# Last block of the down projection: the first product's pairs 9 to 11 behind the second's first two, and the last rows' transposes in front of the seventh's second half

## The chip, the cores and the metric

The kernel runs on one core of a Trainium2 chip. The metric is the device time of one execution in microseconds. Before the change three runs took 992.59, 992.81 and 992.83 us; the median is 992.81.

## What is computed

A decoder trunk of two layers over 512 tokens of width 1024, in float32. Layer 0 mixes tokens with causal pooling, layer 1 with windowed attention; each is followed by a SwiGLU feed-forward block with 2816 hidden features, and a last rmsnorm ends it. Cut to what matters here:

```python
def swiglu(h, w_gate, w_up, w_down):
    g = jnp.einsum('bsd,df->bsf', h, w_gate)
    u = jnp.einsum('bsd,df->bsf', h, w_up)
    return jnp.einsum('bsf,fd->bsd', jax.nn.silu(g) * u, w_down)

def reference(x, ...):
    for i in range(DEPTH):
        h = rmsnorm(x, norm_mix[i])
        y = pool_mixer(h, ...) if i % N_MIXERS == 0 else attn_mixer(h, ...)
        x = x + y
        h = rmsnorm(x, norm_ffn[i])
        x = x + swiglu(h, ffn_w_gate[i], ffn_w_up[i], ffn_w_down[i])
    return rmsnorm(x, norm_final)
```

## The kernel before

**Precision.** Every float32 operand is split into a high part (a cast to fp32r on ScalarE, ACT) and a low part (the difference, on VectorE, DVE). A product is three matmuls: high by high, high by low, low by high. For weights these are L170 (`whi`) and L174 (`wlo`); for activations L360 and L361. The weights' halves live in a ring of five tiles, so a cast waits until TensorE (PE) has finished with the weights five tiles earlier.

**The feed-forward block** (`ffn`, one call for each layer) takes each large matmul as a 2 by 2 block product with seven products instead of eight, numbered 0 to 6. Their operands are sums of blocks. Sums of weights are made by transfers that add to what is there (POOL's, L138 and L179) and by additions on DVE (L176, `vraw<-vraw,wraw`). Sums of activations are made on ACT and DVE.

Gate and up go through eleven groups of 256 hidden features, numbered 0 to 10. Group `n`'s product `i` is `("quad", n, i)` in the plan. Its accumulators are PSUM tiles, `pair0` to `pair3`, which hold two banks each. `paired_done` (L706 to L737) takes a finished product out: L724 and L725 after product 5, L728 and L729 after product 6, then silu and multiplication (L741, L742, L732, L736), the sums of the result (L652, L653, L661), and their split into `u_hi` and `u_lo`. Group 10 keeps its split in two tiles named `t`, which group 10's own operands held before (`open_u`, L641).

Down takes the groups back in three blocks, groups 0 to 2, 3 to 5 and 6 to 10, each again with seven products. Within a block the groups go two by two: a weight tile `z` serves groups `2z` and `2z + 1` of the block. In the last block `z` 0 is groups 6 and 7 (the title's pairs 7 and 8, counted from one), `z` 1 groups 8 and 9 (pairs 9 and 10), `z` 2 group 10 alone (pair 11). `z` 0 and 1 take 12 matmuls of 128x512 each, `z` 2 takes 6. `("down", 2, i, zs)` is product `i` for the tiles in `zs`; a full product is 30 matmuls. Product 0 goes into `pair0` and is copied to `pair2` when complete (L832); product 1 goes into `pair3`, the bank of group 10's product 5.

**What sets the order.** PE follows the order of the program; `_plan` (L52) writes the feed-forward block's part of it. The other engines are ordered by a scheduler from that same program and its priorities, and each then works strictly in its order. The weight queue follows the plan too: a load, cast and split is issued some steps ahead of its use. So a step that moves in the plan moves its load on SP's queue and its cast and split on ACT and DVE.

**Behind the plan**, products 5, 4, 3 and 6 of the last block are written out at the end of `ffn` (L915 to L948) with the residual sum (L840, L842: "flush"), the squares for the next norm (L323), the multiplication by the gain (L332) and the scaling by the inverse root (L351). In layer 0 (`not final`) the normed rows of blocks 2 and 3 are also turned there: `turn_block` does eight 128x128 transposes on PE (L357) and splits the result into `h` (L360, L361), block 2 by way of `pair3`, block 3 by way of `pair2`. Product 6 is done in two halves, rows of block 0 (`first`, 15 matmuls) and of block 1 (`second`, 15 matmuls).

Then layer 1's attention starts with `by_halves` (L1108): three projections for q and k, for the tokens of blocks 2 and 3 first. Between them the transposes of blocks 0 and 1 are put in (L1116), from the row tiles `wraw` and `odd_rows`, which L351 has scaled.

Of the kernel before, what the change touches and what calls it, by code (L numbers as in the profile page):

```python
# [51 lines left out]
def _plan():  # L52
    first = lambda n: [("quad", n, 0)] if n in PAIRED else []
    down = lambda b, i, *zs: ("down", b, i, zs or tuple(range((len(BLOCKS[b]) + 1) // 2)))
    steps = TWO + [("one", 2, i) for i in range(6)] + first(3) + [("one", 2, 6)]
    for n in PAIRED:
        steps += [("quad", n, i) for i in USED]
        ends = [("quad", n, 5), ("quad", n, 6)]
        if n in (3, 6):
            b = n // 3 - 1  # L60
            steps += [down(b, 0)] + ends + [down(b, i) for i in range(1, 6)] + first(n + 1) + [down(b, 6)]
        elif n == 10:
            steps += [down(2, 0, 0, 1)] + ends + [down(2, 1, 0), down(2, 0, 2), down(2, 1, 1, 2)]
            steps += [down(2, i) for i in (2, 5, 4, 3, 6)]
        else:
            steps += first(n + 1) + ends
    return steps


PLAN = _plan()  # L70
TOKENS = np.arange(S).reshape(J, R).T.reshape(-1)
BY_GROUP = [6, 7, 4, 5, 2, 3, 0, 1]
# [3 lines left out]
def trunk_kernel(ctx: ExitStack, tc: tile.TileContext, x_in, xT, gam, gains, consts, ident_d, w0, wT, w1, wv, w_down, out):  # L76
# [290 lines left out]
    def by_residue(b):  # L367

        n = P // R

        def places(h, half, tp):
            at = h[:, 4 * half : 4 * half + 4, :].rearrange("p c (r j) -> p c r j", r=R)
            return at[:, :, :, b * n : (b + 1) * n], tp.rearrange("p c (i r) -> p c r i", r=R)

        return places

    def turned(norm, shift, b, tps, order):

        hi, lo = tokens_at(shift)
        for half, tp in enumerate(tps):  # L380
            norm.turn(b, half, tp)
        for half, tp in enumerate(tps):
            (to_hi, src), (to_lo, _) = order(hi, half, tp), order(lo, half, tp)
            with tc.high_priority(URGENT):
                split(to_hi, to_lo, src)
# [192 lines left out]
    def ffn(layer, norm, third, nxt):  # L578
# [8 lines left out]
        with ExitStack() as fctx:  # L587
# [299 lines left out]
            final = layer == 1  # L887
# [3 lines left out]
            last = downs[2]  # L891
            p, r, _, q = last.accs[:4]
# [20 lines left out]
            turn_block = lambda b, pair: turned(norm, 0, b, [by_four(pair[:, n, :]) for n in range(2)], by_residue(b))  # L913
# [12 lines left out]
            ws = last.operands(6, every)  # L926
            first = last.places(every, (0,))
            last.matmuls(6, ws, first[:4], lambda t: p[:, 0, :], False)
            if not final:
                turn_block(2, r)  # L930
            last.matmuls(6, ws, first[4:], lambda t: p[:, 0, :], False)
            with tc.high_priority(URGENT):
                last.flush(6, p[:, 0:1, :], slice(0, 1))
            closed(1, (0,))
            ready_block(0)
            second = last.places(every, (1,))
            for n, cs in enumerate(HALVES if final else COLS[:1]):
                to = (A[0], r)[n][:, 1, : cs.stop - cs.start]
                if final:
                    last.matmuls(6, ws, second, lambda t: to, True, cs)  # L940
                else:
                    last.matmuls(6, ws, second[:2], lambda t: to, True, cs)
                    turn_block(3, q)
                    last.matmuls(6, ws, second[2:], lambda t: to, False, cs)
                with tc.high_priority(URGENT):
                    last.flush(6, to.unsqueeze(1), slice(1, 2), cs)
                norm.square(1, 1, junk, 2 + n if final else None)
                norm.gained(1, 1, 2 + n if final else None)  # L948
# [5 lines left out]
        return norm  # L954

    norm = ffn(0, norm, third, 1)


    with ExitStack() as actx:
# [24 lines left out]
        def rope(ps, t, name):  # L984
            a = aw.tile([P, S], F32, name="ropea")
            sw = aw.tile([P, S], F32, name="ropeb")
            nc.vector.stream_shuffle(sw, ps, PARTNER)
            nc.vector.tensor_mul(a, ps, cosr)
            nc.gpsimd.tensor_mul(sw, sw, sinr)
            out = aw.tile([P, S], F32, name=name, bufs=3)  # L990

            if t >= 3:
                nc.vector.tensor_add(out, a, sw)
            elif name == "k":
                nc.vector.tensor_add(out.rearrange("p (b r i) -> p b r i", b=4, r=R), blocks_of(a), blocks_of(sw))
            else:
                by_r = lambda z: z.rearrange("p (r j) -> p r j", r=R)
                nc.vector.tensor_add(out.rearrange("p (j r) -> p r j", r=R), by_r(a), by_r(sw))
            return out
# [130 lines left out]
        for t in range(8):  # L1130
            pq = pqk[2 * t] if t < 2 else project(j_qk[2 * t], h_hi, h_lo)
            q = rope(pq, t, "q")
# [172 lines left out]
        third = out_projection(j_wo, range(NC), m_hi, m_lo, norm, SHIFT, four, lambda: [sc_tile(), sc_tile()])  # L1305

    ffn(1, norm, third, 3)
    mm.close()

# [66 lines left out]
```

## Time and profile before

| | |
|---|---|
| median of 3 runs | 992.81 us |
| profiled execution | 993.18 us |
| its span | 991.40 us |
| PE busy | 981.2 us, 99% |
| VectorE busy | 786.3 us, 79% |
| ScalarE busy | 573.7 us, 58% |
| GpSimd busy | 124.5 us, 13% |
| granted TensorE clock | 0.998 |
| read from HBM | 159.85 MB |

The span is what the trace covers, from the first instruction to the end of the last; the profiled execution's own time is 1.78 us longer. PE is TensorE's matmuls, PEld its weight loads, SP the engine that issues most transfers. A row of the timeline gives the start and the length in us, the engine, the line in the code, the operation, what it writes and reads by the program's names, and in brackets the engine's idle time before it and what ended it. A row of stretches gives the bounds, the length and the busy time of the engines with their instructions. The last block of down lies at 385 to 441 us in layer 0 and at 930 to 981 us in layer 1.

### The profile page before, as it was taken

To read this page: it belongs to the slowest core of one execution; us is meant where nothing else is said; L and a number is where in the kernel's file an instruction comes from. 1 tells how busy PE (TensorE), PEld (TensorE's weight loads), DVE (VectorE), ACT (ScalarE), POOL (GpSimd) and SP (SyncE) were. 2 spreads that over 40 slices of the span, in tenths; PEclk is the share of its full clock that TensorE was granted. 3 is DMA by queue.
4 is the path that set the end of the run, shared out by engine and by line. 5 is a ranking of instruction groups with operands and counts; after the bars stand their busy time and mean duration, and the time that the engine had idled before them with its cause. 6 is when DMAs were issued, how large, how long until landed. Compare 5 with 4: busy or idle time off the path is not lost.

```text
span 991.4 us, 15359 instructions
## 1 busy us (share of the span) xinstructions
PE 981.2 (99%) x5914; PEld 869.8 (88%) x5914; DVE 786.3 (79%) x1088; ACT 573.7 (58%) x898; POOL 124.5 (13%) x124
## 2 busy tenths in 40 slices
PE   9999999999999999999999999999999999999997
PEld 7888999988988998789888899899998898899876
DVE  6475789898988888787887547479989798888876
ACT  5573666646765676573543544357664676567655
POOL 0002010010011111102111023101101001110110
PEclk9999999999999999999999999999999999999999
DMA  9557276579469876653211249526757946987662
GB/s 335 181 173 188 52 199 165 137 208 251 127 163 248 216 186 146 149 191 129 85 56 54 61 149 268 116 53 178 199 125 206 254 125 161 249 220 188 139 145 98
DMA packets 79465, 162.98 MB, mean 164 GB/s; under 512 B 6096, under 2 KB 6480, under 8 KB 79392
## 3 DMA queue, kind: packets, MB, share of 16 engines
q1 hardware_dynamic: 58544, 122.04, 37.3%
q0 software_dynamic: 20560, 39.69, 23.3%
q8 instruction: 46, 0.75, 0.3%
q14 instruction: 27, 0.22, 0.1%
q10 hardware_dynamic: 288, 0.27, 0.1%
HBM read 159.85 MB, written 2.13 MB: 163 GB/s over the span
## 4 chain that ended last, share of the span: by engine, by line
PE 93%; DVE 3%; ACT 2%; DMA 1%; issue 1%; POOL 0%; SPq 0%; DVEq 0%; ACTq 0%
PE pair L673 31%; PE pair L817 19%; PE p L699 5%; PE mm L263 4%; PE mm L264 4%; PE mm L265 4%; PE pair L699 4%; PE r L699 2%; PE early L484 2%; PE mm L402 2%; PE mm L404 2%; PE mm L403 2%; PE mm L699 1%; DVE wlo L174 1%; PE early L531 1%; PE tp L1083 1%
## 5 line engine op out<-in xcount | busy, mean ns | idle before, releaser
L174 DVE TENSOR_TENSOR wlo<-wraw,whi 128x1024 fp32r<-128x1024 f32 (+2 forms) x190 | 220.1, 1163 | 70.0 <-ACT whi L170 69.5
L170 ACT CAST whi<-wraw 128x1024 fp32r<-128x1024 f32 (+2 forms) x189 | 184.4, 980 | 155.6 <-issue 28.1
L170 ACT CAST whi<-vraw 128x1024 fp32r<-128x1024 f32 (+1 forms) x108 | 105.4, 980 | 114.7 <-DVE vraw L176 38.1
L174 DVE TENSOR_TENSOR wlo<-vraw,whi 128x1024 fp32r<-128x1024 f32 (+1 forms) x108 | 121.8, 1132 | 44.5 <-ACT whi L170 44.3
L673 PE MATMUL pair<-h,whi 128*128 128x512 f32 (+1 forms) x640 | 143.2, 349 | 0.0
L673 PEld LDWEIGHTS pair<-h,whi 128*128 128x128 f32 x640 | 109.1, 189 | 13.4
L673 PE MATMUL pair<-t,whi 128*128 128x512 f32 (+1 forms) x512 | 110.6, 337 | 0.0
L817 PE MATMUL pair<-whi,u_hi 128*128 128x512 f32 (+1 forms) x284 | 109.9, 387 | 0.0
L817 PE MATMUL pair<-wlo,u_hi 128*128 128x512 f32 (+1 forms) x284 | 109.9, 387 | 0.0
L817 PE MATMUL pair<-whi,u_lo 128*128 128x512 f32 (+1 forms) x284 | 109.7, 386 | 0.0
L673 PEld LDWEIGHTS pair<-t,whi 128*128 128x128 f32 x512 | 86.0, 190 | 8.4
L673 PE MATMUL pair<-h,wlo 128*128 128x256 f32 x512 | 89.2, 281 | 0.0
L673 PEld LDWEIGHTS pair<-h,wlo 128*128 128x128 f32 x512 | 76.1, 188 | 4.2
L138 POOL DMA_DIRECT2D wraw<-w x22 | 26.7, 1211 | 397.5 <-DMA wraw<-w 111.9
L176 DVE TENSOR_TENSOR vraw<-vraw,wraw 128x1024 f32<-128x1024 f32 (+1 forms) x66 | 75.2, 1139 | 0.7
L673 PE MATMUL pair<-t,wlo 128*128 128x256 f32 x384 | 71.9, 282 | 0.0
L263 PE MATMUL mm<-h,whi 128*128 128x512 f32 (+1 forms) x176 | 64.9, 369 | 0.0
L264 PE MATMUL mm<-h,whi 128*128 128x512 f32 (+1 forms) x176 | 63.6, 362 | 0.9 <-DVE h L361 0.9
L265 PE MATMUL mm<-h,wlo 128*128 128x512 f32 (+1 forms) x176 | 63.5, 361 | 0.0
L817 PEld LDWEIGHTS pair<-whi,u_lo 128*128 128x128 f32 x284 | 53.3, 188 | 10.9
L817 PEld LDWEIGHTS pair<-whi,u_hi 128*128 128x128 f32 x284 | 53.4, 188 | 10.4
L817 PEld LDWEIGHTS pair<-wlo,u_hi 128*128 128x128 f32 x284 | 53.4, 188 | 10.3
(346 smaller groups left out, 2043.4 us busy)
## 6 DMA issues: line engine op xcount, KB each, us to landing
wraw<-w SPq DMA_DIRECT2D x116, 512.0 KB, 4.7
wraw<-w_down SPq DMA_DIRECT2D x32, 512.0 KB, 4.1
vraw<-w SPq DMA_DIRECT2D x22, 512.0 KB, 4.9
wraw<-w POOLq DMA_DIRECT2D x22, 512.0 KB, 7.5
vraw<-w POOLq DMA_DIRECT2D x22, 512.0 KB, 9.2
wraw<-wT SPq DMA_DIRECT2D x16, 512.0 KB, 4.2
vraw<-w_down POOLq DMA_DIRECT2D x12, 512.0 KB, 7.4
wraw<-w_down SPq DMA_DIRECT2D x24, 256.0 KB, 3.2
```

What stands on the lines that cost most here:

```text
L138: nc.gpsimd.dma_start(dst, more, accum_op=ALU.add)
L170: nc.scalar.copy(hi[:, :n], raw[:, :n])
L174: nc.vector.tensor_sub(lo[:, :n], raw[:, :n], hi[:, :n].bitcast(F32))
L176: nc.vector.tensor_add(raws[into][:, :n], raws[into][:, :n], raws[more][:, :n])
L263: nc.tensor.matmul(ps, lhsT=whi, rhs=xhi, start=first, stop=False, **kw)
L264: nc.tensor.matmul(ps, lhsT=whi, rhs=xlo, start=False, stop=False, **kw)
L265: nc.tensor.matmul(ps, lhsT=wlo, rhs=xhi, start=False, stop=last, **kw)
L402: nc.tensor.matmul(ps, lhsT=xhi, rhs=w[0][:, k, :], start=first, stop=False)
L403: nc.tensor.matmul(ps, lhsT=xhi, rhs=w[1][:, k, :], start=False, stop=False)
L673: mat = lambda o, w, m, **kw: nc.tensor.matmul(o, lhsT=w, rhs=m, skip_group_check=True, **kw)
L699: nc.tensor.matmul(ps[:, g, :], lhsT=w[:, g, c, :], rhs=right[:, z, c, :], start=i in (0, 1, 3) and g + c + k == 0, stop=c == 3 and k == 2 ...
L817: nc.tensor.matmul(acc(t), lhsT=u, rhs=w, start=first, stop=n == len(places) - 1, skip_group_check=True)
```

## The change

```diff
@@ _plan, n == 10
-            steps += [down(2, 0, 0, 1)] + ends + [down(2, 1, 0), down(2, 0, 2), down(2, 1, 1, 2)]
+            steps += [down(2, 0, 0)] + ends + [down(2, 1, 0), down(2, 0, 1, 2), down(2, 1, 1, 2)]
             steps += [down(2, i) for i in (2, 5, 4, 3, 6)]
@@ ffn, the end
             last.matmuls(6, ws, first[4:], lambda t: p[:, 0, :], False)
+            if not final:
+                turn_block(3, q)
             with tc.high_priority(URGENT):
                 last.flush(6, p[:, 0:1, :], slice(0, 1))
...
                 to = (A[0], r)[n][:, 1, : cs.stop - cs.start]
-                if final:
-                    last.matmuls(6, ws, second, lambda t: to, True, cs)
-                else:
-                    last.matmuls(6, ws, second[:2], lambda t: to, True, cs)
-                    turn_block(3, q)
-                    last.matmuls(6, ws, second[2:], lambda t: to, False, cs)
+                last.matmuls(6, ws, second, lambda t: to, True, cs)
```

`ends` are group 10's products 5 and 6. The first part applies to both layers, the second to layer 0 alone. Lines of the code behind L942 have a number smaller by 3 in the changed kernel. No matmul, transfer, cast or sum is added or taken away.

On PE, at the start of the last block in layer 0 (`pair_1536` is `pair0`, `pair_1539` is `pair3`, `pair_1537` is `pair1`; + is the changed kernel's order), group 10's last two products come after the first weight tile of product 0:

```order
 L817 MATMUL pair_1536<-whi,u_lo 128x512
+L673 MATMUL pair_1539<-h,whi 128x512 x8
+L673 MATMUL pair_1539<-h,wlo 128x256 x8
+L673 MATMUL pair_1537<-t_1001,whi 128x512 x8
+L673 MATMUL pair_1537<-t_1001,wlo 128x256 x8
+L817 MATMUL pair_1539<-whi,u_hi 128x512
+L817 MATMUL pair_1539<-wlo,u_hi 128x512
+L817 MATMUL pair_1539<-whi,u_lo 128x512
```

The four L673 rows and product 1's first 12 matmuls, of which the last three rows are the beginning, stood 12 matmuls later; product 0's second tile now follows them, directly ahead of its third, which reads `t`.

On ACT, at the end of group 10 in layer 0 (L724 and L728 take out products 5 and 6, L360 casts the result into `t`, L735 loads the table for the norm's root), the order was:

```order
L724 COPY ct<-pair_1539 128x512
L741 ACTIVATE ct<-ct 128x2x256
L170 CAST whi<-vraw 128x1024
L728 COPY ct<-pair_1537 128x512
L360 CAST t_999<-ct 128x512
L170 CAST whi<-vraw 128x1024
L732 ACTIVATE ct<-ct 128x256
L735 ACT_TABLE_LOAD
L735 ACTIVATE tiny<-tiny 128x1
L832 COPY pair_1538<-pair_1536 128x1024
L360 CAST t_999<-ct 128x1280
```

and is now:

```order
L724 COPY ct<-pair_1539 128x512
L170 CAST whi<-vraw 128x512
L741 ACTIVATE ct<-ct 128x2x256
L728 COPY ct<-pair_1537 128x512
L732 ACTIVATE ct<-ct 128x256
L735 ACT_TABLE_LOAD
L735 ACTIVATE tiny<-tiny 128x1
L360 CAST t_999<-ct 128x512
L360 CAST t_999<-ct 128x1280
L170 CAST whi<-vraw 128x1024 x2
L832 COPY pair_1538<-pair_1536 128x1024
```

Both casts into `t` stand behind the table load now, and product 2's first two weight casts stand behind both of them.

On ACT, at the end of layer 0's feed-forward block (`pair_1539` holds block 2's turned rows, `pair_1538` block 3's; L323 squares, L351 scales, the L170 rows cast the q and k weights), the order from the first turned half on was:

```order
L360 CAST h<-pair_1539 128x16x32 x2
L170 CAST whi<-wraw 128x1024
L323 ACTIVATE keep,ss<-x 128x512
L360 CAST h<-pair_1538 128x16x32
L338 ACTIVATE s_4153<-ss 128x1
L170 CAST whi<-wraw 128x1024 x2
L360 CAST h<-pair_1538 128x16x32
L351 ACTIVATE wraw<-wraw,r_4154 128x1024
L323 ACTIVATE keep,ss<-x 128x512
```

and is now:

```order
L360 CAST h<-pair_1539 128x16x32
L360 CAST h<-pair_1538 128x16x32
L360 CAST h<-pair_1539 128x16x32
L323 ACTIVATE keep,ss<-x 128x512
L360 CAST h<-pair_1538 128x16x32
L338 ACTIVATE s_4165<-ss 128x1
L170 CAST whi<-wraw 128x1024 x3
L323 ACTIVATE keep,ss<-x 128x512
L351 ACTIVATE wraw<-wraw,r_4166 128x1024
```

The four casts into `h` moved ahead of all three weight casts; the scaling of `wraw` moved behind the third weight cast and behind block 1's square.

## The prediction

> **What bounds the kernel now.** I read the page first: its head, the busy shares and the chain that ended last.
>
> ```profile
> span 991.4 us, 15359 instructions
> PE 981.2 (99%) x5914; PEld 869.8 (88%) x5914; DVE 786.3 (79%) x1088; ACT 573.7 (58%) x898; POOL 124.5 (13%) x124
> ...
> PE 93%; DVE 3%; ACT 2%; DMA 1%; issue 1%; POOL 0%; SPq 0%; DVEq 0%; ACTq 0%
> ```
>
> TensorE (PE) has work for 99% of the span. So a reordering that keeps every matmul can win only where PE now waits, and the next view is who PE waits for over the whole run (us in total, times, longest).
>
> ```profile
> PE mm L264 <- DVE h L361: 0.9, 2, 0.5
> PE pair L817 <- ACT t L360: 0.4, 2, 0.2
> ```
>
> Both rows touch the edit. `t` holds the operands of group 10 that the moved product reads (one wait in each layer), and `h` at L361 is the low half of the turned rows (two waits in layer 0). Idle time understates such a wait, because matmuls are pipelined, so I measure the stretches themselves. The rows below give the stretch, its length, then the busy time of PE, PEld, DVE, ACT and POOL.
>
> ```profile
> 385.02:390.48 5.46, 5.46 (x26) 4.51 (x25) 3.99 (x5) 2.00 (x3) 1.48 (x2) 1.00 0.72 163
> 390.48:396.10 5.62, 5.62 (x34) 4.90 (x32) 4.27 (x6) 3.47 (x5) 0.89 (x2) 1.00 0.89 166
> 396.10:405.22 9.12, 8.76 (x38) 6.61 (x37) 7.04 (x11) 7.03 (x11) 2.40 (x2) 1.00 0.88 191
> 412.02:418.82 6.80, 6.80 (x31) 5.63 (x30) 4.85 (x6) 4.01 (x5) 0.00 (x0) 1.00 0.22 63
> 941.49:950.62 9.13, 8.77 (x39) 6.61 (x38) 7.05 (x11) 6.86 (x10) 2.41 (x2) 1.00 0.87 190
> ```
>
> The first is the first product's two weight tiles (24 matmuls), the second group 10's last two products, the third the 36 matmuls after them, the fourth a product of 30 without any wait. 6.80/30 is 0.227 us a matmul, so 36 should take 8.16 us. They take 9.12 in layer 0 and 9.13 in layer 1: **0.96 and 0.97 us are lost at `t`.**
>
> **Part 1, product 0's later pairs moved.** No matmul, cast or transfer is added or removed. With the same durations PE would stand, on the clock of before, so: 12 matmuls of product 0 from 385.02 to 387.75, group 10's last two to 393.37, 12 of product 1 to 396.10, then pairs 9 and 10 of product 0 to 398.82, and there the first matmul that reads `t`. Its high half is needed at 398.82, its low half two matmuls later at 399.27. Now when `t` is ready:
>
> ```profile
> 393.50 0.59 ACT L724 COPY ct<-pair 128x512 f32<-128x512 f32 x1 [0.33 <-PE pair L673]
> 394.88 0.63 ACT L741 ACTIVATE ct<-ct 128x512 f32<-128x512 f32 x1 [0.80 <-DVE ct L725]
> 396.36 0.58 ACT L728 COPY ct<-pair 128x512 f32<-128x512 f32 x1
> 398.55 0.62 ACT L360 CAST t<-ct 128x512 fp32r<-128x512 f32 x1 [1.60 <-DVE ct L652]
> 400.05 0.41 ACT L732 ACTIVATE ct<-ct 128x256 f32<-128x256 f32 x1
> 400.48 1.28 ACT L735 ACT_TABLE_LOAD   x1
> ...
> 395.48 0.69 DVE L176 TENSOR_TENSOR vraw<-vraw,wraw 128x512 f32<-128x512 f32 x1
> 397.83 0.68 DVE L652 TENSOR_TENSOR ct<-ct 128x512 f32<-128x512 f32 x1
> 398.43 0.68 DVE L729 SCALAR_TENSOR_TENSOR ct<-pair,ct 128x512 f32<-128x512 f32 x1
> 399.37 0.68 DVE L361 TENSOR_TENSOR t<-ct,t 128x512 fp32r<-128x512 f32 x1
> ```
>
> Group 10's last product ends 2.73 us earlier, at 393.37. In the new order ACT does L741 at 393.16, L728 at 393.70 (PE's end plus the 0.2 that L724 shows after 393.30). DVE follows with L742, L729, L652, each 0.60 start to start, L652 ending at 395.7. ACT does L732 at 395.1 and now has the table load and its tiny activation (1.4 us) in front of the cast, which starts at 396.97 and ends at 397.6. DVE reaches the low half at 397.86, behind a 0.62 L176, and ends at 398.55. That is 0.7 us before 399.27, so the wait goes. What is late next would be product 1's first matmul at 393.37, which overwrites the bank that L725 reads: I get L725's end at 392.7, again 0.65 to spare. Spent covers would cost their overrun one for one. Bounds of this step: 0 to 0.97 a layer; I take all of it.
>
> On SP's queue the loads for product 0's second tile and for group 10's last product change places:
>
> ```profile
> 361.27 0.37 SPq L136 DMA_DIRECT2D wraw<-w_down  x1
> ...
> 366.13 0.37 SPq L136 DMA_DIRECT2D wraw<-w  x1
> ```
>
> Even the later of the two lands, at the 7.8 us of the slowest transfer below, 16 us before PE reads either tile (390.57 and 396.10), so the swap costs nothing.
>
> The other weights are the doubtful side. Product 2's splits (L174) fall behind `t`'s larger low half, and each releases the accumulating POOL transfer (L179) that brings product 5's weights.
>
> ```profile
> 398.32 1.19 POOL L179 DMA_DIRECT2D vraw<-w_down  x1 [5.03 <-DVE wlo L174]
> ...
> DMA to landing us min/median/max: 6.6/6.6/6.6
> ...
> 405.06 1.06 ACT L170 CAST whi<-vraw 128x1024 fp32r<-128x1024 f32 x1 [0.46 <-DMA vraw<-w_down]
> ...
> DMA to landing us min/median/max: 7.8/7.8/7.8
> ...
> DMA to landing us min/median/max: 5.7/5.7/5.7
> ```
>
> The landings are of this transfer in layer 0, of its twin in layer 1, and of one of the same size at 377.5 with nothing beside it. Laid out in the new order, the first split of product 2 ends at 401.46 instead of 397.92, and the issue follows 0.4 later (as 398.32 follows 397.92), at 401.85. Landing at 6.6 is 408.5; the cast (1.06), the split (1.23, the L174 row further down) and 0.15 between make 410.9. Product 5 starts at 411.06 and reads the low half one matmul later, 411.29: **no wait, 0.4 to spare.** At 5.7 the spare is 1.3, at 7.8 PE waits 0.76. The last SP load before it moves to 398, so less of it lies beside the transfer than in either layer now; I therefore stay with 6.6. The next two transfers queue behind the first and have 2.7 us each before PE needs them.
>
> The DMA: Bandwidth & Descriptors page of the Trainium skill (SWDGE vs HWDGE vs iDMA) says each DMA engine takes software and hardware queues in turn. 5.7 alone against 6.6 and 7.8 beside loads agrees.
>
> The GPSIMD Engine Reference of the Trainium skill (Specifications) has the POOL engine share its SBUF port with VectorE, in contention when VectorE reads two SBUF inputs; by it the three issues, now in a row beside L174 splits, would stretch. POOL's issue took 1.19 us at 398.32 beside such work, and 1.19 also here, where DVE stood idle for most of it; no stretch shows, and the sum by either is the same unless it reached 0.4 us.
>
> ```profile
> 389.29 1.19 POOL L138 DMA_DIRECT2D wraw<-w_down  x1 [3.98 <-DVE vraw L176]
> 391.76 1.23 DVE L174 TENSOR_TENSOR wlo<-vraw,whi 128x1024 fp32r<-128x1024 f32 x1 [2.28 <-ACT whi L170]
> ```
>
> **Part 2, layer 0's last transposes.** Times stay on the clock of before; all shifts earlier with part 1, since PE frees the buffers that ACT's casts wait for there.
>
> ```profile
> 438.08 1.04 PE L357 MATMUL pair<-ident,ct 128*128 128x128 f32 x8
> ...
> 441.85 0.39 PE L264 MATMUL mm<-h,whi 128*128 128x256 f32 x1 [0.53 <-DVE h L361]
> ...
> 443.99 0.39 PE L264 MATMUL mm<-h,whi 128*128 128x256 f32 x1 [0.34 <-DVE h L361]
> ...
> 445.41 1.03 PE L357 MATMUL tp<-ident,wraw 128*128 128x128 f32 x8
> 446.20 0.36 PE L263 MATMUL mm<-h,whi 128*128 128x256 f32 x1
> ...
> 449.15 1.03 PE L357 MATMUL tp<-ident,odd_rows 128*128 128x128 f32 x8
> ```
>
> From 446.20 to 449.15 the next projection's 24 matmuls take 2.95 us; from 441.04, where this one starts, to 445.41 they take 4.37. So 1.42 us are lost. Moved six matmuls (1.36 us) ahead, the transposes stand at 436.72. DVE does the four splits into `h` 0.60 apart, with the flush at 437.91 (row below), a gain and a tiny step between: they end at 438.0, 439.2, 439.8 and 441.0. PE needs the second at 441.1, and the last 12 matmuls later, at 442.5. Both waits go. But ACT's three QK casts now come before the last square and block 0's scaling:
>
> ```profile
> 437.91 0.67 DVE L842 TENSOR_TENSOR x<-x,pair 128x512 f32<-128x512 f32 x1
> 440.75 1.98 ACT L170 CAST whi<-wraw 128x1024 fp32r<-128x1024 f32 x2
> 443.11 1.16 ACT L351 ACTIVATE wraw<-wraw,r 128x1024 f32<-128x1024 f32 x1
> 444.16 0.62 ACT L323 ACTIVATE keep<-x 128x512 f32<-128x512 f32 x1
> ```
>
> The casts run at 0.95 each from 439.9 to 442.8. On DVE the second flush (L842, as 437.91) comes behind the third QK split, which itself waits for the first of these casts: it runs from 442.37 to 443.05. Then the square starts at 443.08 and block 0's scaling (L351, in before done at 444.27) runs from 443.70 to 444.86. PE reaches block 0's transposes at 441.04 + 2.95 = 443.99 and waits until 444.9, instead of 445.41 in before: **0.5 us is won of the 1.42; 0.9 becomes a new wait, at `wraw`.** Bounds: below nothing, if ACT's queue slips by more than 0.5, and 1.42 at most. Block 1's rows are scaled by about 447.1, and PE comes to them at 448.6, so nothing more is late.
>
> **The sum.** 0.96 + 0.97 + 0.5 = 2.4 us. The profiled execution took 993.18 us (span 991.40), so 990.7 for it; the median shown is 992.81, so **990.4**, or 0.24% less. About 0.2% (2.0 us: below 990.8 or above 994.8) can be told from no change.
>
> **The rivals.**
> - *Block 0's rows are ready in time* (ACT takes the square and the scaling before PE comes). For: PE ends the second product early enough. Against: three casts stand in front. Part 2 then gives 1.42: 992.81 − 0.96 − 0.97 − 1.42 = 989.5. Chance 0.12.
> - *Product 5's weights land late.* For: layer 1's 7.8. Against: fewer loads beside it. At 7.8 PE waits 0.76: 991.1 if in one layer, 991.9 if in both. Chance 0.22.
> - *Part 2 wins nothing*: the new wait at `wraw` eats all of the old one. 990.9. Chance 0.07. This is the case in which the transposes do not do what they were moved for.
> - *Slower*: the same place as the second, with a price that decides. The first L179 transfer would have to take as long as other accumulating transfers into `vraw` do in the middle:
>
> ```profile
> vraw<-w POOLq DMA_DIRECT2D x22, 512.0 KB, 9.2
> ```
>
> At 9.2 it lands at 411.05, the split is done at 413.45, and PE waits 2.16 us in each layer: 990.4 + 4.3 = 994.7. It costs from 7.0 us on, eats the layer's gain at 8.0 and makes the kernel slower by 0.2% from about 9.3. For: three issues now follow each other. Against: those 22 share the engines with loads, which these hardly do. Chance 0.04.
>
> **How the numbers follow.** The forecast has 0.55, with its own range of 989.9 to 990.9, most of it under 990.8 (0.50 of 0.55). With the first rival faster has 0.62; the rest of the forecast and the two middle rivals give 0.34 to no difference; slower has 0.04. The range runs from the first rival's 989.4 to 991.7, which takes in late weights in one layer and most of two.
>
> **What would show it.** Right: the stretch from group 10's last product to product 2 takes 10.9 us (48 matmuls) in both layers with no wait at `t`; the two waits of L264 for `h` are gone; one new wait of about 0.9 us stands before the transposes that read `wraw`, released by ACT's L351. Wrong: a wait at `t` that stays; one at product 5's first matmuls, released by L174 or L170; or transposes of `wraw` that start right after the 24 matmuls.

## The result, and the profile after

| | before | after |
|---|---|---|
| median of 22 runs each | 993.28 us | 991.50 us |
| lowest and highest of them | 992.15, 995.94 | 990.43, 993.99 |
| profiled execution | 993.18 us | 992.38 us |
| its span | 991.4 us | 990.6 us |

The ratio of the times is 0.9982, with a 95% interval of 0.9976 to 0.9989: 0.18% faster, 1.1 to 2.4 us. The forecast was 0.24%, 2.4 us. The size lies at the edge of the interval, and the two profiled executions differ by 0.8 us only. So there are two questions: did each step go as laid out, and where is the rest?

First the head of the changed kernel's page, and then who PE waits for over the whole run (us in total, times, longest).

```profile
span 990.6 us, 15368 instructions
PE 980.2 (99%) x5914; PEld 870.6 (88%) x5914; DVE 785.7 (79%) x1088; ACT 573.2 (58%) x898; POOL 124.6 (13%) x124
```
```profile
PE tp L357 <- ACT wraw L351: 0.9, 1, 0.9
PE mm L1284 <- DVE o L1292: 0.9, 1, 0.9
PE mm L1254 <- DVE v L1260: 0.7, 1, 0.7
```

The rows for `h` at L264 and for `t` are gone. The first row here is the new wait that was forecast, with its size. The second is new and stands in no step of the prediction. The third was there before, in the same view, with 0.5 us:

```profile
PE mm L1257 <- DVE v L1263: 0.5, 1, 0.5
```

The stretches of the changed kernel, from product 1's first matmul to product 2's in layer 0 (48 matmuls), and from block 0's transposes to the second half of block 1's; the columns are those of the prediction.

```profile
393.41:404.31 10.90, 10.90 (x50) 9.02 (x49) 9.51 (x14) 7.82 (x11) 2.46 (x3) 1.00 0.35 108
444.07:448.42 4.35, 4.34 (x36) 4.17 (x36) 4.06 (x7) 2.43 (x5) 0.00 (x0) 1.00 0.70 228
```

10.90 us is the 48 x 0.227 that the prediction gave; in layer 1 it is 10.91 (938.91 to 949.82). Now the timeline of the changed kernel at `t`, on ACT and DVE, and at the first issue that brings product 5's weights.

```profile
397.02 1.77 ACT L360 CAST t<-ct 128x512 fp32r<-128x512 f32 x2
...
397.88 0.68 DVE L361 TENSOR_TENSOR t<-ct,t 128x512 fp32r<-128x512 f32 x1
```
```profile
L179 POOL DMA_DIRECT2D vraw<-w_down x1: 1188/1188/1188, 401.9 to 401.9; - x1
...
DMA to landing us min/median/max: 5.6/5.6/5.6
```

The low half of `t` ends at 398.56 (forecast 398.55; needed by 399.27), the issue stands at 401.85 as laid out, and the transfer lands 5.6 us later, earlier than the 6.6 that was assumed. And the timeline at the end of layer 0's block:

```profile
439.13 2.94 ACT L170 CAST whi<-wraw 128x1024 fp32r<-128x1024 f32 x3
442.26 0.63 ACT L323 ACTIVATE keep<-x 128x512 f32<-128x512 f32 x1 [0.18 <-DVE x L842]
442.89 1.13 ACT L351 ACTIVATE wraw<-wraw,r 128x1024 f32<-128x1024 f32 x1
...
444.07 1.09 PE L357 MATMUL tp<-ident,wraw 128*128 128x128 f32 x8 [0.93 <-ACT wraw L351]
...
447.88 1.20 PE L357 MATMUL tp<-ident,odd_rows 128*128 128x128 f32 x8
```

The queue on ACT is the one forecast: three casts, the square, the scaling, then PE's transposes. They start at 444.07 where before had 445.41.

Matmul by matmul, the changed kernel is 0.9 us ahead of before behind `t`, 1.33 at block 0's transposes (445.41 less 444.07) and 1.16 behind block 1's. By 588 us 0.24 of that is gone, most of it at the longer wait for `v` (0.68 us of idle time against 0.53), and it is 0.92 ahead. But the matmul that starts at 609.69 in before starts at 609.84 here. What happens in between is seen on ACT, DVE and PE of the changed kernel, where layer 1's attention multiplies probabilities and values (L1284) and its result `o` is split into `h`:

```profile
606.28 1.04 ACT L170 CAST whi<-wraw 128x1024 fp32r<-128x1024 f32 x1 [5.06 <-DMA wraw<-w]
607.23 0.62 ACT L360 CAST h<-o 128x512 fp32r<-128x512 f32 x1
...
607.36 1.23 DVE L174 TENSOR_TENSOR wlo<-wraw,whi 128x1024 fp32r<-128x1024 f32 x1 [4.25 <-ACT whi L170]
608.50 0.69 DVE L361 TENSOR_TENSOR h<-o,h 128x512 fp32r<-128x512 f32 x1
609.11 1.28 DVE L1292 TENSOR_TENSOR o<-mm,LB 128x512 f32<-128x512 f32 x2
...
609.84 0.32 PE L1284 MATMUL mm<-pT,v 128*64 128x128 f32 x1 [0.89 <-DVE o L1292]
```

ACT stands idle for 5.06 us with a weight cast at the head of its queue that waits for a load. The weight is the first one of layer 1's gate and up, which PE reads from 660 us on. Behind that cast stands `h<-o`, behind its split on DVE the next `o`, and PE waits for a bank that `o` has to empty. In before the same rows are:

```profile
606.13 1.05 ACT L170 CAST whi<-wraw 128x1024 fp32r<-128x1024 f32 x1 [4.81 <-DMA wraw<-w]
...
607.20 1.23 DVE L174 TENSOR_TENSOR wlo<-wraw,whi 128x1024 fp32r<-128x1024 f32 x1 [3.17 <-ACT whi L170]
608.35 0.68 DVE L361 TENSOR_TENSOR h<-o,h 128x512 fp32r<-128x512 f32 x1
608.95 1.28 DVE L1295 TENSOR_TENSOR o<-mm,LB 128x512 f32<-128x512 f32 x2
```

The load's own rows, of before and then of the changed kernel:

```profile
L136 SPq DMA_DIRECT2D wraw<-w x1: 368/368/368, 595.9 to 595.9; - x1
...
DMA to landing us min/median/max: 10.2/10.2/10.2
```
```profile
L136 SPq DMA_DIRECT2D wraw<-w x1: 367/367/367, 594.9 to 594.9; - x1
...
DMA to landing us min/median/max: 11.2/11.2/11.2
```

So in before the load went out 0.9 us later and the cast still started 0.15 us earlier, and the list of waits names no wait of PE for `o`. But before is held up here too. From the projection's matmuls behind the copies of `v` to the output projection's first matmul PE takes 25.3 us in before (588.47 to 613.77) and 26.4 in the changed kernel (587.55 to 613.92). In each of the nine kernels below that hold the casts back the same matmuls take 24.3. So 1.0 us is lost in before and 2.1 in the changed kernel. In before the matmuls start a little later one after the other, with no idle time between them that the list could name.

The 1.1 us more that the changed kernel loses here is what was left of layer 0's gain, and a little more. What remains is layer 1's 0.95 less the 0.16 by which PE was behind at 609.69, the 0.8 us by which the spans differ. Whether that is a fixed stop or a matter of chance one execution can't tell.

### The profile page after: what moved, and what is told of

The parts are those of the page before. It is cut to its first block, busy times and chain, and to the rows that moved or that the text cites. A ratio compares the mean times of both kernels' runs of the same rounds, so it can differ in the third digit from the quotient of the medians.

```text
span 990.6 us, 15368 instructions
## 1 busy us (share of the span) xinstructions
PE 980.2 (99%) x5914; PEld 870.6 (88%) x5914; DVE 785.7 (79%) x1088; ACT 573.2 (58%) x898; POOL 124.6 (13%) x124
## 5 line engine op out<-in xcount | busy, mean ns | idle before, releaser
L174 DVE TENSOR_TENSOR wlo<-wraw,whi 128x1024 fp32r<-128x1024 f32 (+2 forms) x190 | 220.1, 1163 | 70.3 <-ACT whi L170 69.7
L170 ACT CAST whi<-wraw 128x1024 fp32r<-128x1024 f32 (+2 forms) x189 | 184.0, 979 | 154.1 <-issue 28.1
L170 ACT CAST whi<-vraw 128x1024 fp32r<-128x1024 f32 (+1 forms) x108 | 105.2, 980 | 118.3 <-DVE vraw L176 39.4
L174 DVE TENSOR_TENSOR wlo<-vraw,whi 128x1024 fp32r<-128x1024 f32 (+1 forms) x108 | 121.4, 1131 | 46.2 <-ACT whi L170 46.2
L673 PE MATMUL pair<-h,whi 128*128 128x512 f32 (+1 forms) x640 | 143.2, 349 | 0.0
L673 PEld LDWEIGHTS pair<-h,whi 128*128 128x128 f32 x640 | 109.1, 189 | 13.4
L673 PE MATMUL pair<-t,whi 128*128 128x512 f32 (+1 forms) x512 | 110.6, 337 | 0.0
L673 PEld LDWEIGHTS pair<-t,whi 128*128 128x128 f32 x512 | 86.0, 190 | 8.4
L673 PE MATMUL pair<-h,wlo 128*128 128x256 f32 x512 | 89.2, 281 | 0.0
L673 PEld LDWEIGHTS pair<-h,wlo 128*128 128x128 f32 x512 | 76.1, 188 | 4.2
L673 PE MATMUL pair<-t,wlo 128*128 128x256 f32 x384 | 71.9, 282 | 0.0
L264 PE MATMUL mm<-h,whi 128*128 128x512 f32 (+1 forms) x176 | 63.5, 361 | 0.0
```

Of the source, the lines that this page charges most:

```text
L170: nc.scalar.copy(hi[:, :n], raw[:, :n])
L174: nc.vector.tensor_sub(lo[:, :n], raw[:, :n], hi[:, :n].bitcast(F32))
L264: nc.tensor.matmul(ps, lhsT=whi, rhs=xlo, start=False, stop=False, **kw)
L673: mat = lambda o, w, m, **kw: nc.tensor.matmul(o, lhsT=w, rhs=m, skip_group_check=True, **kw)
```

## The experiments

Each of the three tables below comes from a chip of its own, and before was run beside the other kernels each time.

### The parts alone, and the weight casts held back

The first kernel is the changed one again. The next two take the plan's step alone and the moved transposes alone. The fourth is the changed kernel with ScalarE's casts of layer 1's first four gate and up weights issued behind the last cast of `o`:

```diff
 def weights(...)
-                nc.scalar.copy(hi[:, :n], raw[:, :n])
+                with tc.issue_after(item["cast_behind"]) if "cast_behind" in item else nullcontext():
+                    nc.scalar.copy(hi[:, :n], raw[:, :n])
...
-                split(m_hi[:, t, :], m_lo[:, t, :], o)
+                cast = split(m_hi[:, t, :], m_lo[:, t, :], o)
+        for j in range(j_wo[-1] + 1, j_wo[-1] + 5):
+            queue[j]["cast_behind"] = cast.ins
```

(`split` returns its cast.) It adds a line to the code, so L360 is L361 there.

> The changed kernel once more, as the yardstick on this chip. Theory A (held up in the attention): what layer 0 wins, about 1.1 us, is lost where layer 1's attention value products wait at the second product into o, because ScalarE's cast of the first gate/up weight waits for a load that lands near 606 us whatever TensorE does; only layer 1's 0.9 us stays. A gives 0.8 to 1.3 us less than before, and a wait of about 0.9 us of PE for o. Theory B (the gains carry to the end, the profiled pair was a chance draw): 2.2 to 2.5 us less, no wait at o in most executions.

> Only the plan's step is changed, in both layers; layer 0's transposes stay where they were. By the trace of the changed kernel PE should be 0.9 us ahead of before from 401 us on (no wait for t), and the two waits for h at 441 to 444 us should be back. Theory A: the 0.9 us of layer 0 shrink to 0 to 0.3 at the value products, layer 1's 0.9 stay: 0.9 to 1.2 us less than before. Theory B: 1.9 us less.

> Only layer 0's transposes are moved; the plan's step is as before. PE should be 0.3 to 0.5 us ahead of before behind block 0's transposes (one new wait of about 0.9 us at wraw, released by L351, in place of 1.4 us lost at the two waits for h). Theory A: that is swallowed at the value products, 0 to 0.2 us less in all. Theory B: 0.4 to 0.5 us less.

> The changed kernel, but ScalarE's casts of layer 1's first four gate/up weights stand behind the last cast of the attention's result o (they are read only from 660 us on). Nothing else moves on PE, SP and POOL. Theory A: the wait for o at the value products goes, and layer 0's 1.1 us come through to the end: 1.9 to 2.4 us less than before, 0.9 to 1.3 less than the changed kernel. Theory B: the same as the changed kernel within 0.3 us.

| kernel | median, us | lowest and highest, us | ratio to before, 95% |
|---|---|---|---|
| before (26 runs) | 993.90 | 991.50, 995.75 | |
| changed kernel (11) | 991.63 | 989.65, 992.95 | 0.9976 (0.9967 to 0.9985) |
| plan's step alone (10) | 991.54 | 990.18, 992.95 | 0.9974 (0.9965 to 0.9984) |
| transposes alone (11) | 992.98 | 992.07, 994.79 | 0.9994 (0.9985 to 1.0003) |
| changed, casts held (6) | 990.27 | 989.89, 990.75 | 0.9963 (0.9951 to 0.9975) |

One more run of the transposes alone took 3400.38 us and is not in its row; it was the profiled one, so that kernel has no profile to read. The gain of that kernel, 0.9 us by the medians and -0.3 to 1.5 by the interval, decides nothing.

Theory A, a fixed stop that keeps only layer 1's gain, falls: the plan's step alone wins 2.4 us (1.6 to 3.5 by the interval), not 0.9 to 1.2. Theory B, that the gains simply carry, fails on the fourth kernel: held casts take another 1.4 us off the changed kernel, 3.6 less than before and more than either theory gave, and the spread of single times shrinks from 3.3 to 0.9 us. The wait is real but its length is drawn anew in each execution. The traces show the draw, the time from issue to landing of that one load: 11.2 us in the changed kernel's execution above. In the first kernel here, the changed one again, and then in the one with held casts it was:

```profile
DMA to landing us min/median/max: 9.5/9.5/9.5
```
```profile
DMA to landing us min/median/max: 12.5/12.5/12.5
```

The first of these executions has no row for `o` among PE's waits and loses 0.3 us there by the count of matmuls. Its span is 988.0 us, 2.6 less than that of the execution shown above of the very same kernel: 1.8 of it at `o`, 0.6 at `v` and 0.3 at the start of the run. In the second the load landed at 607.86, and nothing minded: ACT's cast of the first `o` ran at 603.58, as soon as DVE had made it.

```profile
603.58 0.62 ACT L361 CAST h<-o 128x512 fp32r<-128x512 f32 x1 [1.93 <-DVE o L1294]
605.87 0.62 ACT L361 CAST h<-o 128x512 fp32r<-128x512 f32 x1 [1.68 <-DVE o L1294]
```

### The control, and two more waits

If the wait is a draw, before must pay for it as well. That is the first kernel here: before with the casts held. The second attacks the forecast wait at `wraw`. The third attacks the wait for `v` at 587 us, which the changed kernel's DVE rows put down to a tiny transfer:

```profile
585.48 0.18 DVE L1194 TENSOR_TENSOR den<-den,mx 128x24 f32<-128x24 f32 x1 [4.09 <-DMA mx<-gw]
585.59 0.83 DVE L174 TENSOR_TENSOR wlo<-wraw,whi 128x640 fp32r<-128x640 f32 x1
586.33 0.88 DVE L1260 COPY v<-mm 128x320 f32<-128x320 f32 x2
...
586.87 0.41 PE L1254 MATMUL mm<-whi,h 128*128 128x320 f32 x1 [0.68 <-DVE v L1260]
```

A multiplication of 0.18 us that waits for a transfer stands in front of the copies of `v` for which PE waits. The fourth kernel has all three repairs.

```diff
 second kernel, in weights()
+            if item.get("gate"):
+                break
 behind ready_block(0)
+            if not final:
+                queue[j_qk[2]].pop("gate")
+                for j in j_qk[2:4]:
+                    queue[j]["cast_behind"] = norm.scaled.ins
 third kernel
-            merge(0, back)
+            with tc.issue_after(out_of[0].ins):
+                merge(0, back)
```

(`norm.scaled` is the L351 of block 0, `out_of[0]` the last copy of `v` into place on DVE.)

> The kernel before, with nothing of the change, but with the casts of layer 1's first four gate/up weights behind the last cast of o, as in the run that held them for the changed kernel. Theory A' (that cast waits for a load that takes 9.5 to 12.5 us from issue to landing, a different time in each execution, and costs either kernel; the profiled execution of before, with 10.2, was one without a visible wait): 0.8 to 2.0 us less than before, and a spread of single times of about 1 us in place of 4. Theory C (only a kernel that comes to the value products earlier than before runs into this wait): 0 to 0.4 us less.

> The changed kernel with the held casts, and in layer 0's end the third, fourth and fifth q/k weight casts behind block 0's scaling (L351) on ScalarE, so that the scaling no longer stands behind them. If the new wait of part 2 at wraw is made by those casts, as the prediction had it, it shrinks from 0.9 to 0.1 to 0.4 us and the kernel takes 0.5 to 0.8 us less than the changed kernel with the held casts alone: 3.9 to 4.6 us less than before. Rival: the scaling is late because its inverse root comes late on VectorE, or the third projection now waits for its weights: the same within 0.3 us, a wait of about 0.9 us at wraw or at the third projection.

> The changed kernel with the held casts, and VectorE's small multiplication by the first group's share (merge of group 0, which waits for four tiny transfers through GpSimd's queue) behind the copies of v that free PE's banks. If it is that wait which holds PE at 587 us (0.5 to 0.9 us for v, different in each execution), it goes: 0.4 to 0.8 us less than the changed kernel with the held casts. Rival: the weight split behind the multiplication or the copies themselves are what is late: the same within 0.3 us, the wait for v stays.

> The changed kernel with all three repairs (held casts, scaling ahead of the q/k casts, merge behind the copies of v). If the three waits are independent, their gains add: 4.5 to 5.2 us less than before, 988.7 to 989.4 us on this chip if before takes 993.9 there. If one repair only uncovers another, no better than the best of the single ones.

| kernel | median, us | lowest and highest, us | ratio to before, 95% |
|---|---|---|---|
| before (18 runs) | 993.27 | 991.97, 997.01 | |
| before, casts held (12) | 992.27 | 991.86, 993.21 | 0.9985 (0.9974 to 0.9996) |
| changed, casts held, scaling first (7) | 990.29 | 989.30, 990.96 | 0.9960 (0.9945 to 0.9975) |
| changed, casts held, merge behind (6) | 989.65 | 989.41, 989.87 | 0.9954 (0.9937 to 0.9970) |
| changed, all three (6) | 988.95 | 988.31, 989.05 | 0.9945 (0.9929 to 0.9962) |

The ratios are not the quotients of the medians: 988.95/993.27 would be 0.9957.

Theory C falls: before pays too, 1.0 us by the medians (0.4 to 2.6 by the interval, which only touches C's 0.4), and its single times close up from 5.0 to 1.4 us. Its profiled execution, with 10.2 us for the load, was expected to be one without a visible wait. The list of waits indeed shows none, but by the count of matmuls it loses 1.0 us at `o`, which the kernel with the casts held does not. That is the profile that the prediction was made from.

Scaling first gave nothing in the median when added to the held casts (0.9960 against 0.9963, on two chips and with wide intervals), a miss; but with the merge behind the copies as well, it takes 0.70 us off (988.95 against 989.65, spreads of 0.5 to 0.7 us), inside the 0.5 to 0.8 expected. The traces show the gain in both pairs. PE is idle for 0.04 us or less where it waited for `wraw`, and behind block 1's transposes it has gained 0.77 us with the held casts and 0.71 with the merge behind as well. So the forecast wait is made as the prediction says, and in the times winning it back showed only where the draw at `v` no longer blurred it. The merge behind the copies takes 0.6 us off the held casts by the medians of two chips, inside the 0.4 to 0.8 expected. All three repairs stand 4.3 us below before by the medians, a little short of the 4.5 to 5.2 expected. The waits of PE in the kernel with all three are these, at the start of the run and in a projection of the attention, none in the edited stages:

```profile
PE mm L305 <- DVE odd_rows L299: 1.1, 1, 1.1
PE mm L1266 <- ACT ropea L1252: 0.3, 1, 0.3
PE early L489 <- ACT h L464: 0.2, 1, 0.2
```

With the merge behind, DVE's copies run as soon as PE has the products, ahead of the transfer:

```profile
584.97 0.49 DVE L1265 COPY v<-mm 128x320 f32<-128x320 f32 x1 [0.39 <-PE mm L1261]
585.63 0.18 DVE L1196 TENSOR_TENSOR den<-den,mx 128x24 f32<-128x24 f32 x1 [0.17 <-DMA mx<-gw]
```

### The change on a quiet base

With the casts held and the merge behind, a kernel's single times agree within 1 us, so the terms of the sum can be measured one by one. Four kernels: before so repaired, with the plan's step, with the transposes, and with both.

> The kernel before with the two waits of the attention repaired (held casts, merge behind the copies of v), as a quiet base for the three that follow. From the single repairs: 0.3 to 0.9 us less than with the held casts alone, 991.4 to 992.0 us, single times within 1 us.

> The quiet base with the plan's step alone. The prediction's terms (0.96 and 0.97 us, nothing given back): 1.9 us less than the quiet base. Rival (a part of it is given back at other waits, as the pair with held casts, 2.0 us for both parts, allows): 1.4 to 1.7 us less.

> The quiet base with layer 0's moved transposes alone. The prediction's term: 0.5 us less than the quiet base (1.42 less 0.9 of new wait). Rival by the trace of the changed kernel, in which PE stands only 0.25 to 0.45 us further ahead of before behind the turned rows than in front of them: 0.2 to 0.4 us less.

> The quiet base with the whole change. The prediction's sum: 2.4 us less than the quiet base. Rival (the two pairs of runs with held casts): 2.0 us less. If parts 1 and 2 are independent it is the sum of the two runs before this one, within 0.3 us.

| kernel | median, us | lowest and highest, us | less than the quiet base | forecast |
|---|---|---|---|---|
| quiet base (11) | 991.69 | 991.28, 991.77 | | |
| plan's step (5) | 989.72 | 989.36, 989.86 | 1.97 | 1.93 |
| transposes (11) | 991.33 | 990.85, 991.70 | 0.36 | 0.5 |
| both (5) | 989.50 | 989.12, 989.81 | 2.19 | 2.4 |

Before itself took 993.92 us beside these (21 runs, 991.87 to 995.88): the two repairs alone are worth 2.2 us (the base lies inside the 991.4 to 992.0 expected; ratio 0.9978, 0.9969 to 0.9987), as much as the change, and take the spread from 4.0 to 0.5 us. The plan's step is worth what was forecast to 0.04 us; that lies above its rival's 1.4 to 1.7. The transposes are worth less, 0.36 alone, inside their rival's 0.2 to 0.4. On top of the step they are worth 0.22: five runs each, with single times that overlap, so this figure alone is not clear of noise. The whole, 2.19, lies between the 2.4 forecast and the rival's 2.0, and the two parts by themselves add up to 2.33.

## Why the prediction was right, and where it was off

- **The waits at `t`** were the right size (0.96 and 0.97 us) and nothing was late next. Measured on the quiet base the step gives 1.97 for 1.93. The forecast times of the layout (cast at 396.97, low half at 398.55, issue at 401.85) were met to 0.05 us.
- **Product 5's weights**, the likeliest rival, did not come late. The assumed 6.6 us was too long: in the nine profiled executions that had the plan's step, both layers, the first of the three transfers took 5.6 to 6.0 us (18 landings), and 7.0 would have been needed to cost anything. But the reason given, fewer loads beside it, is not needed. In the three later kernels without the plan's step (before with the casts held, the quiet base, the transposes on it) the same transfer at its old place took 5.7 to 6.2 us, so the 6.6 and 7.8 of before's one profile were long ones. The Trainium skill states in its GPSIMD Engine Reference (Specifications) that GpSimd shares its SBUF interfaces with VectorE, with contention when VectorE reads two SBUF inputs. No cost of that shows here: beside the weight splits the first issue took 1188 ns, the 1.19 us of before. The second and third took 1.29 and 1.49 us; whether VectorE or the issue just ahead of them made them longer is not shown, and PE waited for none.
- **The transposes' new wait** came where and as large as said: 0.93 us, released by L351. On the clock of before, PE's transposes start at 444.99 (444.07 and the 0.92 by which all is ahead there), forecast 444.9. The gain at that point is 0.41 (1.33 less 0.92), forecast 0.5.
- **"Block 1's rows are scaled by about 447.1, and PE comes to them at 448.6, so nothing more is late"** is the step that failed, by 0.17 us. The rows were in time, but the bank was not. Block 1's transposes took 1.20 us where before took 1.03 (the last timeline row above), so that the second stretch above took 4.35 us where before took 4.17 (445.41 to 449.58); the tile view of the changed kernel, for `tp` from 447.8 to 449 us, names who was waited for and who waited:

```profile
  DVE h L361: 0.2, 1
who waited for it (us, times):
...
  PEld tp L357: 0.2, 1
```

  DVE's two splits of block 0's turned rows start at 447.08, behind two weight splits (L174) from 444.83 on, and end at 448.36; the fifth transpose of block 1, the first into the second bank, starts at 448.42. In before the splits ended at 449.36 and that transpose started at 449.58. The prediction counted the rows that the transposes read and not the bank that they write. With it the term is 0.41 less 0.17, 0.24, which agrees with the 0.22 to 0.36 measured. The traces of the two quiet pairs, with and without the transposes, say the same: PE gains 0.43 and 0.41 us up to block 0's transposes and keeps 0.26 and 0.24 behind block 1's.
- **The sum** of 2.4 became 2.19 on the quiet base: 0.04 more for the step, 0.14 to 0.28 less for the transposes.
- **What the prediction did not see** is that two places behind the edit, both in layer 1's attention, are set by when a transfer lands and not by PE: the weight cast ahead of `o` at 606 us, and the multiplication ahead of the copies of `v` at 586 us. They cost before 2.2 us in the median, and with them its times vary by some 4 us from run to run. The profile that the prediction read had already lost 1.0 us at `o` and 0.8 at `v` (against the kernels with both repaired), where its list of waits shows 0.5. So the 1.78 us measured first (1.1 to 2.4) and the 2.27 us of the second set (993.90 less 991.63) agree with the 2.19 of the quiet base, and the 0.8 us between the two profiled executions is a gain of about 2.1 less the 1.3 more that the changed kernel's lost there.
- **The time itself** owes something to luck. The forecast started from 992.81, the median of three runs, where 22 runs had 993.28. The 991.50 measured lies above the 989.9 to 990.9 that the forecast alone was given, and inside the whole range only because that reached to 991.7 for product 5's weights coming late, which they did not.

Not settled: what makes the load take 8 us in one execution and 12 in another was not tried, and only the changed kernel was profiled twice (11.2 and 9.5 us). The ten broadcasts issued beside it (`LB<-far` and `even_rows<-far`, from 592.54 on in the changed kernel) are there in all of them.

## What to carry to other kernels

An engine that works in order turns an early cast of a weight nobody needs yet into a wait for whatever stands behind it. Before sizing a change of 0.2%, look in the profile for such operations that wait for a transfer just ahead of something PE needs: the list of waits may show none there though the matmuls lose 1 us, and the next execution loses 0.3 or 2. Count matmul by matmul from one execution to the other. Repairing them first gave a base on which terms of 0.3 us could be measured with a handful of runs, and was worth as much as the change. When a transpose is moved, count the bank that it writes like the rows that it reads.

## What the hardware showed that was not expected

One and the same 512 KB load (the gate and up weight issued at 594 to 596 us) took from 8.1 to 12.5 us from issue to landing in the 13 profiled executions; the median of all 116 loads of its kind and size in the changed kernel is 4.8. The shortest was that of the kernel with all three repairs:

```profile
DMA to landing us min/median/max: 8.1/8.1/8.1
```

The first of product 5's three accumulating transfers, equally large, stayed within 5.6 to 6.0 us in 18 landings of the nine executions with the plan's step; the second and third, issued 1.1 and 1.9 us behind it, took 7.1 to 8.9.
